# Attention maxima as one paced stream, P @ V two pieces behind its scores, and four gate tiles kept for the first merges, in a hybrid encoder layer

## The chip, the core and the metric

The kernel runs on one core of one Trainium2 chip. The metric is the device time of one execution in microseconds (us); a lower number is better. The engines are PE (TensorE, matrix products), DVE (VectorE), ACT (ScalarE), POOL (GpSimd) and SP (SyncE, which here only issues the DMAs). Each engine works through its own queue in order, and waits where an operand or a buffer isn't ready.

## What is computed

One encoder layer over 1280 tokens (1024 of a sample, 256 of a prompt), all in fp32. Cut to what matters here:

```python
h = rms_norm(x, g);  proj = h @ w_in          # split into the three mixers and three gate logits
# A: 8-head latent attention, non-causal, per request group
s = einsum('bqhd,bkhd->bhqk', q, k) * scale;  o_a = (softmax(s) @ v) @ w_o_a
# B: bidirectional RWKV-7, a scan over time for 8 heads of 64
o_b = (groupnorm(y_f + y_b) * g7) @ w_o_b
# C: 4-head attention into 256 memory tokens
o_c = (softmax(xq @ mk.T * scale) @ mv) @ w_o_c
merged = sigmoid(gate_0) * o_a + sigmoid(gate_1) * o_b + sigmoid(gate_2) * o_c
x = x + merged @ w_out
x = x + ConvFFN(rms_norm(x))
```

## The kernel before

Every fp32 product that must be exact is done as three fast products: an operand is split into a high and a low part (ACT casts the high part, POOL subtracts it for the low one, line 126 and 129), and `mm3` (lines 133 to 135) adds high*high, low*high and high*low. The 1280 tokens lie in three chunks `CH` of 512, 512 and 256 columns, numbered `ci` 0, 1, 2.

The program has two phases. Phase 1 projects h for all mixers and writes what attention and the scan need to memory. Phase 2 runs the RWKV scan (chunked into ten groups of tiles, `z` 0 to 9) with other work between its matmuls, then merges the three branches, then the output projection and the FFN.

In the first half of phase 2 the order of PE's queue is written by a planner, `Order`. Three lanes (`rwkv_chain`, `rwkv_inverse`, `rwkv_pairs`) say when their next matmuls can be ready, in planned microseconds of PE time; where none is ready, the planner takes a piece from `fill`, and when that is empty from `spare`. `fill` is first attention (a generator that yields after each piece), then the 24 gate tiles of chunk 1 (`gates`). `spare` are 16 gate tiles of chunk 0 in the list `g0`. A gate tile is 24 matmuls into one bank (PSUM tile `gt`), an evacuation by DVE (`go`, line 879) and a DMA to memory.

Of each `z` the lanes do this: for four pairs, `rwkv_decay` (PSUM tile `zz`), the Gram products (`gram`, line 1452) and the transposes (`bkt`, lines 1477 and 1480); then an inverse, most of it on DVE (from the transpose `R`, line 1507, to `P2w`, line 1562), and its products on PE (`pn`, `i`, `i32t`, then `dp` and `dd`); then two steps of the chain. A step of the chain is three groups of matmuls named `ch` (lines 1290, 1315, 1327), each of which waits for copies by ACT or DVE of the one before, with the outputs `yp` beside them.

Attention goes by items: 8 heads times 3 chunks, then 4 memory heads times 3 chunks. An item of chunk 0 or 1 has 8 pieces (blocks of 128 keys), one of chunk 2 has 2. A piece is three score matmuls (`st`, a bank of the pool `pat` with three buffers), an Exp on ACT (`pf`, line 1106), and the product with V (`ao`, line 1071; fp32, so two rows each in the profile). Scores are shifted by each query's maximum, which is found two items earlier by `neg_max`: a rough score matmul (`mx`, line 936, a bank of the same pool) and a maximum on DVE (line 937), 8 of them for an item of chunk 0 or 1, 2 for one of chunk 2; the result goes by DMA into a row of the query tile.

For each item `more()` makes two generators: `a` loads the keys and queries of the item three ahead, `b` finds the maxima of the item two ahead. After each piece `step(1)` advances both by one; after the item's last piece `rest()` runs both to their ends. The product of a piece stands in the list `late` with count 1: `unit()`, called after the next piece's Exp is issued, emits it.

The merges (`merges`) take attention's result first: `merge_in` loads four tiles (`mf`, and the reciprocals `mrd`), scales them on DVE (line 1693) and splits them into `moh`, `mol`. For each of eight output tiles `m`, `merge` multiplies with `w_o` (`woh`, `wol`, PSUM tile `mg_ps`) and applies the gate; between them stand `rwkv_out` (one of ten token tiles of the scan's output, on DVE, ACT and POOL, with four transposes `yt` on PE, line 1662), a gate tile that is kept on chip, and `gate0()`, which takes a tile that is left in `g0`. `rwkv_out` of tiles 8 and 9 stands between the merges of attention and those of the memory branch.

Of the kernel before, what the change touches and what calls it, by code (L numbers as in the profile page):

```python
# [97 lines left out]
class Kern:  # L98
# [801 lines left out]
    def spare(self, ctx, pp):  # L900

        self.gates_h(ctx[1], 0)
        self.mid = False
        yield -8.0
        while self.g0:
            self.mid = True
            for x in self.gate_(ctx[1], pp, "at", self.g0.pop(0), 0, "go", 3):
                if isinstance(x, float):
                    yield x
            self.mid = False  # L910
            yield 512 * 2.4 / 1024
# [47 lines left out]
    def attention(self, pm, tag):  # L959

        nc, io = self.nc, self.io
        with self.pool("att", side="right") as p:
# [35 lines left out]
            def ahead(h, ci):  # L998
                c0, cn = CH[ci]
                if ci == 0:  # L1000
                    e = 65 * (h % 2)
                    nc.sync.dma_start(
                        out=v1[:, :, e : e + 64], in_=io["vA"][:, :, h * 64 : (h + 1) * 64].rearrange("i p f -> p i f")
                    )
                qh, ql = queries()
                ks = []
                for c in {0: (0, 1), 1: (), 2: (2,)}[ci]:
                    cs = slice(CH[c][0], CH[c][0] + CH[c][1])
                    ks.append((io["kaT"][h][:, cs], *(k[:96, cs] for k in keys(h))))
                nxt.append((qh, ql))  # L1010
                ms = (0, NS) if c0 < NS else (NS, T)
                args = qh[:96, :cn], keys(h)[0][:96], ms, cn // 128, (qh[96:97, :cn], ql[96:97, :cn])
                mxs.append(args)
                yield from loads(*ks, (io["qT"][h][:, c0 : c0 + cn], qh[:96, :cn], ql[:96, :cn]))

            def x_ahead(h, ci):
# [10 lines left out]
                nxt.append((qh, ql, nm, self.onesr[r : r + 2]))  # L1027
                a = 0 if c0 < NS else 256
                mxs.append((qh[:, :cn], x_keys(h)[0], (a, a + 256), cn // 128, (nm[0:1, :cn], nm[1:2, :cn])))
                yield from loads(*ks)  # L1030
# [3 lines left out]
            nxt, mxs = [], []  # L1034
            for n, g in enumerate(itertools.islice(aheads, self.LOOK)):
                for _ in g:
                    pass
                if n < self.LOOK - 1:
                    for _ in self.neg_max(p, pm, tag, *mxs.pop(0)):
                        pass  # L1040
                yield
            pm, tag, po = self.pa, "at", self.po

            def more():

                a = next(aheads, iter(()))
                b = self.neg_max(p, pm, tag, *mxs.pop(0)) if mxs else iter(())

                def step(n):
                    for x in (a, *(b,) * n):  # L1050
                        next(x, None)

                def rest():
                    for x in (a, b):
                        for _ in x:
                            pass

                return step, rest
            late = []
# [33 lines left out]

            for x, h, ci in items[:24]:
                qh, ql = nxt.pop(0)
# [3 lines left out]
                ot = []  # L1099
                step, rest = more()  # L1100
                for n, kt in enumerate(kts):
# [7 lines left out]
                    args = ot, slice(0, 65), cn, v1[:, kt, e : e + 65], pf[:, :cn], kt == kts[0], kt == kts[-1]  # L1109
                    late.append([1, lambda args=args: product(*args)])  # L1110
                    if kt == kts[-1]:
                        late.append([1, lambda args=(ot, h, c0, cn): put_a(*args)])
                    step(1)
                    yield cn * 3.6 / 1024
                rest()
            while late:
                unit()
            self.recips(0, 8)
            for x, h, ci in items[24:]:
                qh, ql, nm, one = nxt.pop(0)  # L1120
# [4 lines left out]
                ot, pfs = [], []  # L1125
                step, rest = more()
                for kt in kts:
# [10 lines left out]
                    if kt == kts[-1]:  # L1138
                        late.append([1, lambda args=(ot, h, c0, cn): put_c(*args)])
                        late.append([1, lambda a=pfs[0][:, :cn], b=pfs[1][:, :cn]: nc.gpsimd.tensor_add(out=a, in0=a, in1=b)])  # L1140
                        late.append([2, lambda args=(pfs[0], h, c0, cn): den_c(*args)])
                    step(2)
                    yield cn * 4.4 / 1024
                rest()
            while late:
# [263 lines left out]
    def rwkv_prep(self, p, pr, gr, j, st):  # L1409
# [45 lines left out]
        for e in range(2):  # L1455
# [4 lines left out]
            for q in range(2):  # L1460
# [6 lines left out]
                )  # L1467
        self.od.pe(1.2, "pr", 2.7)
        yield
# [255 lines left out]
    def merges(self, gp, ro, mg, pp, merged):  # L1725
# [358 lines left out]
```

## Time and profile before

| | us |
|---|---|
| Median of three runs | 3017.24 (3015.17 to 3018.32) |
| Profiled execution, its own time | 3016.91 |
| Its span, first to last instruction | 3015.1 |
| PE busy in the span | 2796.7 (93%) |
| DVE busy | 1546.9 (51%) |
| POOL busy | 1352.4 (45%) |
| ACT busy | 1173.7 (39%) |

The profile gives, for one execution, the busy time of each engine, and in stretches of the span the clock that was granted to TensorE (1 is 2.4 GHz, 0.5 is 1.2 GHz, a figure between them is the mean of a stretch). A timeline has one row for a run of like instructions: start, length, engine, line, tile written and tiles read, and in square brackets the idle time just before it with what ended it. A view of waits adds such idle times by pair of waiter and releaser. Lengths of matmuls overlap, since they are pipelined; the distance between two starts is what a matmul costs the queue.

### The profile page before, as it was taken

To read this page: it belongs to the slowest core of one execution; us is meant where nothing else is said; L and a number is where in the kernel's file an instruction comes from. 1 tells how busy PE (TensorE), PEld (TensorE's weight loads), DVE (VectorE), ACT (ScalarE), POOL (GpSimd) and SP (SyncE) were. 2 spreads that over 40 slices of the span, in tenths; PEclk is the share of its full clock that TensorE was granted. 3 is DMA by queue.
4 is the path that set the end of the run, shared out by engine and by line. 5 is a ranking of instruction groups with operands and counts; after the bars stand their busy time and mean duration, and the time that the engine had idled before them with its cause. 6 is when DMAs were issued, how large, how long until landed. Compare 5 with 4: busy or idle time off the path is not lost.

```text
span 3015.1 us, 50261 instructions
## 1 busy us (share of the span) xinstructions
PE 2796.7 (93%) x19556; PEld 2244.5 (74%) x19556; DVE 1546.9 (51%) x2576; ACT 1173.7 (39%) x2561; POOL 1352.4 (45%) x1220
## 2 busy tenths in 40 slices
PE   6998998998888988989989598999999999999999
PEld 5787787885555665567767476888888888888888
DVE  8638858665666566755665365423423223233233
ACT  5645454635545545554443233433221111211111
POOL 5546636453433433545544366843433332433322
PEclk9999998998989989999989799999999999999999
DMA  4233224553122222243333665532111111111112
GB/s 152 95 97 104 86 79 119 137 149 83 46 54 55 60 55 68 78 136 106 106 118 103 183 190 167 167 97 72 44 37 36 43 35 43 36 42 39 34 38 84
DMA packets 250005, 261.77 MB, mean 87 GB/s; under 512 B 81028, under 2 KB 178448, under 8 KB 249768
## 3 DMA queue, kind: packets, MB, share of 16 engines
q1 hardware_dynamic: 249768, 258.57, 29.1%
q8 instruction: 154, 2.52, 0.3%
q14 instruction: 83, 0.68, 0.1%
HBM read 196.64 MB, written 61.73 MB: 86 GB/s over the span
## 4 chain that ended last, share of the span: by engine, by line
PE 43%; DVE 3%; DMA 3%; issue 2%; POOL 2%; ACT 1%; SPq 1%; DVEq 0%; POOLq 0%; ACTq 0%
PE up L133 7%; PE up L134 7%; PE up L135 7%; PE dn L133 3%; PE dn L134 3%; PE dn L135 3%; PE gt L133 2%; PE gt L134 1%; PE gt L135 1%; PE wo_ps L133 1%; PE wo_ps L135 1%; PE wo_ps L134 1%; DMA mg<-s_gT 1%; POOL w4l L129 1%; PE mg_ps L134 1%
## 5 line engine op out<-in xcount | busy, mean ns | idle before, releaser
L133 PE MATMUL up<-h2h,wuh 128*128 128x512 f32 (+1 forms) x1056 | 374.2, 354 | 0.0
L134 PE MATMUL up<-h2h,wul 128*128 128x512 f32 (+1 forms) x1056 | 374.0, 354 | 0.0
L135 PE MATMUL up<-h2l,wuh 128*128 128x512 f32 (+1 forms) x1056 | 373.5, 354 | 0.0
L129 POOL TENSOR_TENSOR w4l<-w4f,w4h 128x512 fp32r<-128x512 f32 (+1 forms) x154 | 265.2, 1730 | 210.9 <-ACT w4h L126 197.5
L129 POOL TENSOR_TENSOR wul<-wuf,wuh 128x1024 fp32r<-128x1024 f32 x52 | 125.1, 2406 | 270.4 <-ACT wuh L126 270.4
L133 PEld LDWEIGHTS up<-h2h,wuh 128*128 128x128 f32 x1056 | 199.7, 189 | 27.9
L135 PEld LDWEIGHTS up<-h2l,wuh 128*128 128x128 f32 x1056 | 199.6, 189 | 27.8
L134 PEld LDWEIGHTS up<-h2h,wul 128*128 128x128 f32 x1056 | 199.7, 189 | 27.4
L1832 DVE TENSOR_TENSOR x<-x,dn 128x512 f32<-128x512 f32 (+1 forms) x192 | 113.6, 598 | 194.3 <-PE dn L135 194.3
L133 PE MATMUL proj<-hh,w4h 128*128 128x512 f32 (+1 forms) x504 | 181.8, 362 | 9.0 <-DVE go L879 5.0
L134 PE MATMUL dn<-ah,wdl 128*128 128x256 f32 (+1 forms) x528 | 187.2, 356 | 0.0
L135 PE MATMUL dn<-al,wdh 128*128 128x256 f32 (+1 forms) x528 | 184.7, 356 | 0.0
L133 PE MATMUL dn<-ah,wdh 128*128 128x256 f32 (+1 forms) x528 | 182.1, 356 | 0.4 <-ACT wdh L126 0.4
L134 PE MATMUL proj<-hh,w4l 128*128 128x512 f32 (+1 forms) x504 | 180.5, 358 | 1.1 <-POOL w4l L129 1.1
L135 PE MATMUL proj<-hl,w4h 128*128 128x512 f32 (+1 forms) x504 | 180.9, 359 | 0.0
L133 PE MATMUL gt<-ghh,w4h 128*128 128x512 f32 x384 | 162.5, 423 | 13.0 <-ACT w4h L126 6.0
L1071 PE MATMUL ao<-pf,va 128*65 128x512 f32 (+1 forms) x288 | 152.8, 614 | 22.8 <-ACT pf L1106 15.1
L126 ACT CAST wuh<-wuf 128x1024 fp32r<-128x1024 f32 x52 | 54.7, 1051 | 291.3 <-PE up L135 276.1
L1852 DVE TENSOR_TENSOR fraw<-up,rbc 128x512 f32<-128x512 f32 (+1 forms) x66 | 39.8, 604 | 247.7 <-PE up L135 241.0
L126 ACT CAST w4h<-w4f 128x512 fp32r<-128x512 f32 (+1 forms) x154 | 113.2, 750 | 136.5 <-DMA w4f<-in_w_g 35.4
L129 POOL TENSOR_TENSOR wdl<-wdf,wdh 128x384 fp32r<-128x384 f32 (+1 forms) x64 | 60.3, 944 | 225.1 <-ACT wdh L126 225.1
L134 PE MATMUL gt<-ghh,w4l 128*128 128x512 f32 x384 | 154.8, 403 | 5.0 <-POOL w4l L129 5.0
(392 smaller groups left out, 7382.5 us busy)
## 6 DMA issues: line engine op xcount, KB each, us to landing
w4f<-in_w_g SPq DMA_DIRECT2D x48, 512.0 KB
wuf<-in_w_up SPq DMA_DIRECT2D x44, 512.0 KB
rk<-s_rk SPq DMA_DIRECT2D x80, 192.0 KB
w4f<-in_w_g SPq DMA_DIRECT2D x48, 256.0 KB
s_gT<-go SPq DMA_DIRECT2D x40, 256.0 KB
mg<-s_gT SPq DMA_DIRECT2D x40, 256.0 KB
wdf<-in_w_down SPq DMA_DIRECT2D x48, 192.0 KB
w4f<-in_w_rw SPq DMA_DIRECT2D x30, 256.0 KB
```

Source lines behind the costliest of these rows:

```text
L126: nc.scalar.copy(out=hi, in_=x)
L129: (nc.gpsimd if el == "pool" else nc.vector).tensor_sub(out=lo, in0=x, in1=hi.bitcast(F32))
L133: mm(ps, lhsT=lh, rhs=rh, start=first, stop=False)
L134: mm(ps, lhsT=ll, rhs=rh, start=False, stop=False)
L135: mm(ps, lhsT=lh, rhs=rl, start=False, stop=last)
L1071: nc.tensor.matmul(ot[0][out, :cn], lhsT=lhsT, rhs=rhs, start=start, stop=stop)
L1832: nc.vector.tensor_add(out=xc, in0=xc, in1=ps[:, :cn])
L1852: nc.vector.tensor_mul(out=raw[:, o : o + cn], in0=ps, in1=self.rbc[:, c0 : c0 + cn])
```

## The change

Six edits:

1. `more()` with its `step` and `rest` is gone. One stream runs the maxima of all items: `step(a, n)` advances the loads by one and adds n to a credit (at most 2), and each whole credit advances the running `neg_max` by one maximum, whichever item it belongs to. n is 1.15 per piece of the heads and 2.0 per piece of the memory heads. `ready(i)` runs the stream as far as item i needs before its first piece.
2. An item's maxima are entered in the list `mxs` after its loads are issued, no longer before, and the DMA for V follows the loads.
3. A product and what follows it (`put_a`) stand in `late` with count 2 instead of 1, for the eight heads; the memory heads keep 1.
4. The first pair of the scan is planned at 9.0 us instead of 0, and the bank of a Gram product is held 3.4 planned us instead of 2.7.
5. `spare` stops while four tiles are left in `g0`, and the merges take these four before the first `merge_w`.
6. `rwkv_out` of tiles 8 and 9 moves behind the start of the first two merges of the memory branch.

```diff
-        while self.g0:
+        while len(self.g0) > 4:
...
+                yield from loads(*ks, (io["qT"][h][:, c0 : c0 + cn], qh[:96, :cn], ql[:96, :cn]))
                 mxs.append(args)
-                yield from loads(*ks, (io["qT"][h][:, c0 : c0 + cn], qh[:96, :cn], ql[:96, :cn]))
+                if ci == 0:
+                    e = 65 * (h % 2)
+                    nc.sync.dma_start(
...
-            def more():
-
-                a = next(aheads, iter(()))
-                b = self.neg_max(p, pm, tag, *mxs.pop(0)) if mxs else iter(())
...
+            pace = [0.0, None]
+
+            def step(a, n):
+
+                next(a, None)
+                pace[0] = min(pace[0] + n, 2.0)
+                while pace[0] >= 1.0:
+                    if pace[1] is None:
+                        if not mxs:
+                            return
+                        pace[1] = self.neg_max(p, pm, tag, *mxs.pop(0))
+                    try:
+                        next(pace[1])
+                        pace[0] -= 1.0
+                    except StopIteration:
+                        pace[1] = None
+                        done.append(0)
+
+            def ready(i):
+
+                while len(done) <= i:
+                    pace[0] = 1.0
+                    step(iter(()), 0.0)
...
-                    late.append([1, lambda args=args: product(*args)])
+                    late.append([2, lambda args=args: product(*args)])
                     if kt == kts[-1]:
-                        late.append([1, lambda args=(ot, h, c0, cn): put_a(*args)])
-                    step(1)
+                        late.append([2, lambda args=(ot, h, c0, cn): put_a(*args)])
+                    step(a, 1.15)
                     yield cn * 3.6 / 1024
-                rest()
+                for _ in a:
+                    pass
...
-                    step(2)
+                    step(a, 2.0)
...
-                yield "pr", lambda: 0.0 if z < 2 else od.when(f"c{z - 2}")
+                yield "pr", lambda: (0.0 if n else 9.0) if z < 2 else od.when(f"c{z - 2}")
...
-        self.od.pe(1.2, "pr", 2.7)
+        self.od.pe(1.2, "pr", 3.4)
...
         for m in range(8):
+            if m == 0:
+                for _ in range(4):
+                    gate0()
             w = self.merge_w(mg, 0, m)
...
-        self.rwkv_out(ro, pp, 8)
-        self.rwkv_out(ro, pp, 9)
         for m in range(8):
+            if m < 2:
+                self.rwkv_out(ro, pp, 8 + m)
```

What this does to the queues, at three places. First, PE at the end of an item of chunk 2, here the second head's. Before (`st` are scores, `ao` products with V, `mx` maxima, `zz` and `gram` belong to the scan):

```order
L133 MATMUL st<-aqh,akb_5961 128x256
L134 MATMUL st<-aqh,akb_5961 128x256
L135 MATMUL st<-aql,akb_5961 128x256
L1071 MATMUL ao<-pf,va 65x256
L936 MATMUL mx<-akb_5960,aqh 128x512 x7
L133 MATMUL st<-aqh,akb_5960 128x512
L134 MATMUL st<-aqh,akb_5960 128x512
L135 MATMUL st<-aql,akb_5960 128x512
L1071 MATMUL ao<-pf,va 65x256
```

The same place of PE's queue now:

```order
L133 MATMUL st<-aqh,akb_5960 128x256
L134 MATMUL st<-aqh,akb_5960 128x256
L135 MATMUL st<-aql,akb_5960 128x256
L1081 MATMUL ao<-pf,va 65x512
L936 MATMUL mx<-akb_5961,aqh 128x256 x2
L133 MATMUL st<-aqh,akb_5961 128x512
L134 MATMUL st<-aqh,akb_5961 128x512
L135 MATMUL st<-aql,akb_5961 128x512
L1081 MATMUL ao<-pf,va 65x256
```

The seven maxima in a row are gone (there were seven such rows in the program, and now there is no row of more than two behind the start of phase 2), and the product behind a piece is that of two pieces before.

Second, PE at the end of the scan, from the last two groups of its last chain to the first merge (`gt` are gate tiles). Before:

```order
L133 MATMUL gt<-ghh,w4h 128x512
L1327 MATMUL ch_17982<-W,bkt 64x64 x16
L1336 MATMUL yp<-W,g_16189 64x64 x4
L1336 MATMUL yp<-W,g_16190 64x64 x4
L1336 MATMUL yp<-W,g_16191 64x64 x4
L1336 MATMUL yp<-W,g_16192 64x64 x4
L134 MATMUL gt<-ghh,w4l 128x512
L135 MATMUL gt<-ghl,w4h 128x512
L133 MATMUL gt<-ghh,w4h 128x512
L134 MATMUL gt<-ghh,w4l 128x512
L135 MATMUL gt<-ghl,w4h 128x512
L133 MATMUL mg_ps<-moh,woh 128x512
```

And now, from the last chain's last step on:

```order
L1304 MATMUL ch_17916<-W,agr 64x64 x16
L1312 MATMUL yp<-sd,agr 64x128 x8
L1329 MATMUL ch_17947<-xs,Tt_6469 64x64 x16
L1341 MATMUL ch_17966<-W,bkt 64x64 x16
L1350 MATMUL yp<-W,g_16257 64x64 x4
L1350 MATMUL yp<-W,g_16258 64x64 x4
L1350 MATMUL yp<-W,g_16259 64x64 x4
L1350 MATMUL yp<-W,g_16260 64x64 x4
L133 MATMUL gt<-ghh,w4h 128x512
L134 MATMUL gt<-ghh,w4l 128x512
L135 MATMUL gt<-ghl,w4h 128x512
```

From the last `dp` to the first merge there were 87 gate matmuls, between the chain's groups; now there is none among them, and four tiles (96 gate matmuls, ten merge matmuls among the last of them) follow the last `yp`. Three tiles (72 matmuls) that stood in the merges of `m` 0, 1 and 2 are gone from there, and 63 more gate matmuls stand ahead of that `dp`.

Third, POOL at the entry of the merges (`w4l` splits a gate tile's weights, `mol` and `wol` the merges' operands). Before:

```order
L129 TENSOR_TENSOR w4l<-w4f,w4h 128x1024 x3
L129 TENSOR_TENSOR mol<-mf,moh 128x256
L129 TENSOR_TENSOR wol<-wof,woh 128x512
L129 TENSOR_TENSOR mol<-mf,moh 128x512
L129 TENSOR_TENSOR mol<-mf,moh 128x256
L129 TENSOR_TENSOR mol<-mf,moh 128x512
```

And now:

```order
L1318 TENSOR_TENSOR sw<-sd,wc 64x512 x2
L129 TENSOR_TENSOR mol<-mf,moh 128x256
L129 TENSOR_TENSOR wol<-wof,woh 128x512
L129 TENSOR_TENSOR w4l<-w4f,w4h 128x1024
L129 TENSOR_TENSOR mol<-mf,moh 128x512
L129 TENSOR_TENSOR w4l<-w4f,w4h 128x1024
L129 TENSOR_TENSOR mol<-mf,moh 128x256
```

The weights of the third and fourth kept tile are split between the first tiles of attention's result.

## Rows read from the trace of the kernel before

**Rows 1.** Busy time by stretch of the span: heads, and entry of the merges.
```profile
core 0: us, PE busy (x) PEld busy (x) DVE busy (x) ACT busy (x) POOL busy (x), PEclk, DMA share, GB/s
684.20:1184.50 500.30, 448.63 (x4307) 289.25 (x4308) 316.85 (x707) 265.37 (x777) 192.46 (x204) 0.91 0.22 57
...
1683.40:1728.20 44.80, 12.11 (x27) 6.42 (x25) 18.29 (x30) 10.94 (x20) 17.82 (x15) 0.55 0.72 213
```

**Rows 2.** Waits of PE from 676 to 1184.5 us, largest pairs.
```profile
engine line waited for: us in total, times, longest us
PE mx L936 <- DVE m L937: 16.4, 11, 3.3
PE ao L1071 <- ACT pf L1106: 15.1, 19, 2.6
PE zz L1372 <- DMA lt<-s_lora: 7.7, 1, 7.7
...
PE ao L1071 <- DVE P2w L1562: 3.6, 1, 3.6
```

**Rows 3.** The seven rows of seven maxima, by stretch: line 936 alone.
```profile
core 0: us, PE busy (x) PEld busy (x), PEclk, DMA share, GB/s
...
780.20:789.60 9.40, 4.18 (x7) 2.08 (x7) 0.66 0.31 91
...
sum 44.70, PE 26.24 PEld 14.15; mean PE 3.75 PEld 2.02
```

**Rows 4.** Timeline of PE: a piece with a maximum, one without.
```profile
763.21 0.48 PE L133 MATMUL st<-aqh,akb 97*128 97x512 f32 x1
...
763.99 1.02 PE L1071 MATMUL ao<-pf,va 128*65 128x512 f32 x2
764.45 0.79 PE L936 MATMUL mx<-akb,aqh 96*128 96x512 f32 x1
765.08 0.40 PE L133 MATMUL st<-aqh,akb 97*128 97x512 f32 x1
...
696.59 0.80 PE L133 MATMUL st<-aqh,akb 97*128 97x512 f32 x1
...
698.15 0.80 PE L133 MATMUL st<-aqh,akb 97*128 97x512 f32 x1
```

**Rows 5.** The six stretches at half clock that begin in such a row.
```profile
855.00:868.60 13.60, 12.59 (x33) 7.86 (x34) 12.05 (x48) 4.82 (x12) 0.73 (x1) 0.50 0.35 84
...
sum 57.80, PE 50.86 PEld 33.02 DVE 47.94 ACT 13.62 POOL 17.23; mean PE 8.48 PEld 5.50 DVE 7.99 ACT 2.27 POOL 2.87
```

**Rows 6.** Three of five items of chunk 1, a maximum behind each piece.
```profile
705.40:726.00 20.60, 19.53 (x109) 12.22 (x105) 12.07 (x22) 13.68 (x43) 10.16 (x11) 1.00 0.17 46
754.60:776.40 21.80, 20.19 (x111) 12.22 (x110) 18.94 (x53) 14.17 (x49) 9.53 (x11) 1.00 0.14 43
...
1085.40:1121.30 35.90, 34.71 (x622) 25.49 (x620) 19.48 (x36) 21.69 (x66) 12.63 (x16) 1.00 0.15 39
```

**Rows 7.** Timeline: a chain step of the ninth group, then the last chain.
```profile
1596.87 1.15 PE L1290 MATMUL ch<-W,agr 128*64 128x64 f32 x32
...
1599.92 1.15 PE L1315 MATMUL ch<-xs,Tt 64*64 64x64 f32 x32
...
1603.28 1.15 PE L1327 MATMUL ch<-W,bkt 128*64 128x64 f32 x32
...
1605.98 0.42 DVE L1286 COPY W<-sd 64x512 f32<-64x512 f32 x1
...
1655.91 1.15 PE L1290 MATMUL ch<-W,agr 128*64 128x64 f32 x32 [0.30 <-DVE Tt L1627]
...
1681.30 1.10 PE L1336 MATMUL yp<-W,g 128*64 128x64 f32 x32
...
1728.18 1.12 PE L1662 MATMUL yt<-ident,oy 128*128 128x128 f32 x4 [3.56 <-DVE oy L1658]
```

**Rows 8.** Timeline of PE: one gate tile, first row and the row behind it.
```profile
1738.81 0.39 PE L133 MATMUL gt<-ghh,w4h 128*128 128x512 f32 x1
...
1744.29 0.39 PE L133 MATMUL mg_ps<-moh,woh 128*128 128x512 f32 x1
```

**Rows 9.** Timeline of PE: the transposes of the tenth token tile.
```profile
1867.82 1.12 PE L1662 MATMUL yt<-ident,oy 128*128 128x128 f32 x4 [11.29 <-DVE oy L1658]
```

**Rows 10.** Timeline of POOL: the low part of one gate tile's weights.
```profile
1684.96 2.34 POOL L129 TENSOR_TENSOR w4l<-w4f,w4h 128x1024 fp32r<-128x1024 f32 x1 [5.28 <-ACT w4h L126]
```

More of the change, by code (lines that the diff above doesn't have):

```diff
@@ L999, in ahead @@
                 c0, cn = CH[ci]
[L1000 to L1004, printed above, removed]
                 qh, ql = queries()
@@ L1012, in ahead @@
                 args = qh[:96, :cn], keys(h)[0][:96], ms, cn // 128, (qh[96:97, :cn], ql[96:97, :cn])
+                yield from loads(*ks, (io["qT"][h][:, c0 : c0 + cn], qh[:96, :cn], ql[:96, :cn]))
                 mxs.append(args)
-                yield from loads(*ks, (io["qT"][h][:, c0 : c0 + cn], qh[:96, :cn], ql[:96, :cn]))
+                if ci == 0:
+                    e = 65 * (h % 2)
+                    nc.sync.dma_start(
+                        out=v1[:, :, e : e + 64], in_=io["vA"][:, :, h * 64 : (h + 1) * 64].rearrange("i p f -> p i f")
+                    )
             def x_ahead(h, ci):
@@ L1028, in x_ahead @@
                 a = 0 if c0 < NS else 256
+                yield from loads(*ks)
                 mxs.append((qh[:, :cn], x_keys(h)[0], (a, a + 256), cn // 128, (nm[0:1, :cn], nm[1:2, :cn])))
-                yield from loads(*ks)
             items = [(x, h, ci) for x, n in ((0, 8), (1, 4)) for h in range(n) for ci in range(3)]
             aheads = iter([(x_ahead if x else ahead)(h, ci) for x, h, ci in items])
-            nxt, mxs = [], []
+            nxt, mxs, done = [], [], []
             for n, g in enumerate(itertools.islice(aheads, self.LOOK)):
@@ L1040, in attention @@
                         pass
+                    done.append(0)
                 yield
             pm, tag, po = self.pa, "at", self.po
-            def more():
-                a = next(aheads, iter(()))
-                b = self.neg_max(p, pm, tag, *mxs.pop(0)) if mxs else iter(())
[L1049 to L1058, printed above, removed]
+            pace = [0.0, None]
[12 more added lines that the diff above has]
+                        pace[1] = None
+                        done.append(0)
+            def ready(i):
+                while len(done) <= i:
+                    pace[0] = 1.0
+                    step(iter(()), 0.0)
             late = []
@@ L1092, in den_c @@
                 nc.sync.dma_start(out=io["den"][8 + h : 9 + h, c0 : c0 + cn], in_=ds[0:1, :cn])
-            for x, h, ci in items[:24]:
+            for i, (x, h, ci) in enumerate(items[:24]):
+                ready(i)
                 qh, ql = nxt.pop(0)
@@ L1099, in attention @@
                 ot = []
-                step, rest = more()
+                a = next(aheads, iter(()))
                 for n, kt in enumerate(kts):
@@ L1118, in attention @@
             self.recips(0, 8)
-            for x, h, ci in items[24:]:
+            for i, (x, h, ci) in enumerate(items[24:], 24):
+                ready(i)
                 qh, ql, nm, one = nxt.pop(0)
@@ L1125, in attention @@
                 ot, pfs = [], []
-                step, rest = more()
+                a = next(aheads, iter(()))
                 for kt in kts:
@@ L1141, in attention @@
                         late.append([2, lambda args=(pfs[0], h, c0, cn): den_c(*args)])
-                    step(2)
+                    step(a, 2.0)
                     yield cn * 4.4 / 1024
-                rest()
+                for _ in a:
+                    pass
             while late:
```

## The prediction

> **What bounds the kernel now.** I read four things in this order. The time by stretch comes first: PE is busy nearly all the time, so what can be won is where it isn't, or where its clock is low. In the heads' stretch, 500.3 us, PE is busy for 448.6 and has a mean clock of 0.91 [rows 1]. At the entry of the merges, 44.8 us, it is busy for 12.1 at 0.55 [rows 1]. The rest of the span is not touched, and I leave it as it is. Second, the waits in the heads: PE waits 16.4 us for DVE's maxima, 15.1 for the Exp of a piece before its product, 7.7 once for the first load of the scan [rows 2]. Third, the rows of seven maxima, where the first of these waits sits: seven of them take 44.7 us [rows 3]. Fourth, the clock beside them: of the stretches at half clock in the heads, six, together 57.8 us, begin in one of these rows [rows 5], while five items of chunk 1, in which a maximum follows each piece, ran at 1.00 throughout [rows 6]. So PE's own queue sets the time here, through bursts that DVE can't keep up with and through the clock behind them.
>
> The sum is made against the profiled execution's 3016.9 us (its span and 1.8 beside it), which is 0.3 below the median of the three runs; about 0.2%, 6 us, is what a measurement of this kernel can tell from no change.
>
> **The change part by part.**
>
> *The start.* PE waits 7.73 us for the scan's first load [rows 2]. Planned at 9 us, that load's matmuls stand behind four attention pieces, whose inputs were loaded in phase 1. What then hides it is the pieces; if their banks come free late it is hidden in part. Between 0 and -7.7 I take **-6.5**.
>
> *The paced maxima.* A piece with a maximum takes 765.08 - 763.21 = 1.87 us, one without 698.15 - 696.59 = 1.56 [rows 4]: a maximum between pieces costs 0.31. The 49 maxima of the seven bursts, 44.7 us [rows 3], then cost 49 x 0.31 = 15; those that stand in twos cost a little more, so -29 becomes **-26**. If DVE is as late for spread maxima as for bunched ones, nothing comes of it; the ends are 0 and -29.
>
> *The clock.* A mean of 0.91 over 500.3 us [rows 1] is 90 us at half clock, which cost at most half of that. Of the 57.8 us that begin in bursts [rows 5], some 21 lie in the bursts (counted above) and 36 behind them, so 18 us were lost there. I take 14 of these, and 4 for the low stretch that begins in the wait at the start: **-18**, with ends of -5 and -35 (then the other low stretches go too). What rows say for it: the items with a maximum behind each piece kept 1.00, with PE busy 19.5 of 20.6 us and 34.7 of 35.9 [rows 6].
>
> The Trainium skill has a rule that speaks against this (TensorE: Matmul & The Clock Gate, section "A second HAM failure mode: psum-queue depth-cycling"): a kernel that cycles through PSUM banks in each iteration idles in small gaps often enough that the clock swings between its two levels. Scores and maxima do cycle through three banks here. By that rule this term would be 0; by the row it is -18. The trace disagrees with the rule for this pattern: 1.00 in all five items.
>
> *P @ V two pieces behind.* The product no longer waits for the Exp just issued; 15.1 us of such waits in 19 places [rows 2]. But the pool has three banks, and scores and maxima take them in turn: the maximum behind piece n+1 takes the bank of piece n, and so waits for the same Exp, only a product later, 764.45 - 763.99 = 0.46 us [rows 4]. So each wait shrinks by 0.46 at most and moves from `ao` to `mx`: 19 x 0.46 = 8.7, less the waits that were smaller, **-7**; ends 0 and -15.
>
> *The fuller queues.* What is won from PE's queue makes DVE and ACT denser: DVE was busy 316.9 of 500.3 us in the heads [rows 1], and in one item during an inverse 18.9 of 21.8 [rows 6]. Each piece now hangs on a maximum, also in the pieces of chunk 0, which mostly had none while DVE did the inverse. The nearest row is PE's one wait for the inverse, 3.6 us [rows 2]; at two or three such waits for the five groups that lie in the heads, I add **+12**, ends 0 and +30.
>
> *Longer hold of a Gram bank, loads before maxima, V behind the loads.* Pieces are 1.8 planned us, so a hold of 2.7 or 3.4 is mostly two pieces either way; the V load on SP's queue waits for a product that is two pieces later, with 8 pieces to spare. I cost these at nothing; what covers them is attention itself.
>
> *The last chain and the entry.* A gate tile is 1744.29 - 1738.81 = 5.48 us [rows 8], 0.228 a matmul. The order has 63 more gate matmuls ahead of the last `dp`: +14.4. The last chain took 1681.30 - 1655.91 = 25.4 us with gates in it [rows 7]. Bare, a step is about 2.0 to its second group (the 3.05 of the rows less the Gram product that stood between), 3.36 to the third, and 3.1 to the end of the copy for the next step [rows 7], 8.5 in all; to the last `yp` it is 8.5 + 2.0 + 3.4 + 1.0 = 14.9. So the chain ends 14.4 - 10.5 = 3.9 later in PE's work. From there to the first `yt` it was 46.9 us, nearly all loading [rows 7]; the loads start at the chain's end as before, and the four tiles, 22 us, now lie under them. POOL gets two splits of 2.34 between the merges' own [rows 10]: up to +4.7, I take +2. Then three tiles, 3 x 5.48 = 16.4, no longer stand in the merges; as the merges behind them get shorter their own loads show, and I give back 2. Sum 3.9 + 2 - 16.4 + 2, about **-9**; ends -16 and +6.
>
> *Token tiles 8 and 9.* PE stood 11.29 us before the second one's transposes [rows 9]. Now 24 merge matmuls stand ahead of them, some 4.6 us of work that is done inside the wait; what is late next is the last tiles of the memory branch, so **-3.5**, ends 0 and -4.6.
>
> Sum: -6.5 - 26 - 18 - 7 + 12 - 9 - 3.5 = **-58**, so 3016.9 - 58 = **2959 us**.
>
> **The rivals.**
>
> *DVE takes the place of the burst.* DVE's queue is in order, and a maximum behind the inverse's operations is late for each piece and not only in a burst. For it: 18.9 of 21.8 us busy in an item [rows 6]. Against it: that same item lost hardly anything, with PE busy 20.2 of 21.8. Then the pacing gives half, the later product nothing, and the fuller queues cost 24: -58 + 13 + 7 + 12 = -26, **2991 us**.
>
> *The clock stays as it is.* Three banks in turn make small gaps everywhere, and the heads stay at 0.91: without the clock's 18 and with 3 more for the slower start, -37, **2980 us**. Against it stands 1.00 in five items [rows 6]. This is what the rule named above gives.
>
> *More comes than I count.* All low stretches of the heads go (-35), the Exp waits too (-15), nothing is given back by DVE: -58 - 17 - 8 - 12, and a bit less at the ends, **2922 us**.
>
> *Slower.* The inverse itself becomes the bound. Its DVE operations stand in order with the maxima, thirteen or so of them in its time; if they stretch it beyond PE's time from `R` to `pn`, PE stands before `pn`, and the chain, the pairs and the loads behind it with it. It decides from about 12 us per group over five groups on top of the 12 I count, plus the clock lost in each gap: 58 + 15, **3032 us**. Against it: one single wait of 3.6 us for the inverse in the heads [rows 2].
>
> **How the numbers follow.** My forecast has 0.62, DVE's place 0.17, the clock 0.05, more 0.10, slower 0.06. The forecast's own range is 2935 to 2985. The range 2922 to 2997 takes in the clock's case, most of DVE's and part of the better one; it leaves out slower (0.06) and about 0.12 at the two ends. Faster by over 0.2%: the first four less the far end of DVE's, 0.91; within it 0.03; slower 0.06.
>
> **What would show it.** After the change the waits `mx` for DVE should be under 6 us in the heads, the clock there 0.97 or more, the wait for the scan's first load gone, Exp waits partly under `mx`. The heads' stretch, 500.3 us [rows 1], should take some 460. At the entry PE should be busy for 30 us or more, and the last chain should show gaps of 1 to 2 us between its groups. The longest wait of `yt` should fall below 8. I am wrong if the low stretches stay without the bursts, if `st` or `mx` wait for DVE in each item, or if the wait for the inverse comes back in each group.

## The result and the profile after

The changed kernel takes 2967.78 us (median of four runs, 2966.98 to 2974.26); the kernel before, measured beside it, 3016.66. The ratio is 0.9843, with a 95% interval of 0.9825 to 0.9860: 49 us less, where 58 were forecast. The profiled run has a span of 2966.6 us.

The stretches, PE alone (length, busy time and instructions, mean granted clock, DMA): from the end of phase 1 to the start of the scan, heads, memory heads, gates up to the last `dp`, last chain, from there to the first `yt`, merges.

```profile
670.60:681.30 10.70, 7.41 (x29) 1.00 0.67 195
681.30:1126.60 445.30, 410.45 (x4176) 0.95 0.24 63
1126.60:1248.30 121.70, 111.09 (x1028) 0.86 0.26 76
1248.30:1627.00 378.70, 350.23 (x4180) 0.94 0.37 113
1627.00:1647.70 20.70, 12.90 (x354) 0.92 0.17 53
1647.70:1698.60 50.90, 29.39 (x123) 0.81 0.72 220
1698.60:1935.90 237.30, 220.23 (x1073) 0.96 0.60 178
```

The same stretches of the kernel before:

```profile
676.40:684.20 7.80, 0.07 (x3) 0.79 1.00 293
684.20:1184.50 500.30, 448.63 (x4307) 0.91 0.22 57
1184.50:1297.70 113.20, 103.35 (x1207) 1.00 0.28 81
1297.70:1651.10 353.40, 325.00 (x3834) 0.94 0.38 114
1651.10:1682.40 31.30, 31.00 (x435) 1.00 0.32 100
1682.40:1728.20 45.80, 13.11 (x31) 0.56 0.71 210
1728.20:1984.40 256.20, 233.76 (x1145) 0.97 0.57 171
```

Start and heads together went from 508.1 to 456.0 us (-52.1), the memory heads from 113.2 to 121.7 (+8.5, at a clock of 0.86 that was 1.00), the gates from 353.4 to 378.7 (+25.3), the last chain from 31.3 to 20.7 (-10.6), the way to the first `yt` from 45.8 to 50.9 (+5.1), the merges from 256.2 to 237.3 (-18.9). Phase 1 was 5.8 shorter; what follows the merges took 1030.7 in both. Not all of the heads' 52 us is won: in the gates' stretch PE has 346 instructions more. 63 of them are gate matmuls; the others are one inverse's products (256) and a pair's decay and transposes (28), which used to lie among the attention's pieces; by the distances between such groups in the timeline they are some 9 us of work. Only a part of that stood in the heads: with 16 Gram products that went into the memory heads, some 5 us. The rest left the memory heads, which have 179 instructions less and still take longer.

What PE waited for in the heads, largest pairs (to be read against [rows 2]):

```profile
engine line waited for: us in total, times, longest us
PE ao L1081 <- ACT os L1085: 13.7, 7, 5.2
PE mx L936 <- DVE m L937: 8.0, 5, 3.0
PE st L133 <- ACT pf L1117: 6.4, 5, 2.1
PE zz L1386 <- DMA lt<-s_lora: 3.3, 1, 3.3
```

The waits of a product for its Exp are gone from the list (15.1 us before). In their place stands a pair that was small in the kernel before, a product for `os`:

```profile
PE ao L1071 <- ACT os L1075: 3.8, 3, 2.3
```

There is one bank for `ao`; ACT empties it into `os` when an item is done, and the next item's first product needs it. The longest of these waits, on ACT:

```profile
1119.34 0.38 ACT L1117 ACTIVATE pf<-st 128x256 f32<-128x256 f32 x1
1123.93 0.20 ACT L1477 COPY dblk<-gram 32x64 f32<-32x64 f32 x1 [4.22 <-DVE agr L1473]
...
1124.58 0.58 ACT L1085 COPY os<-ao 65x512 f32<-65x512 f32 x1
```

And on PE at the same time:

```profile
1119.19 0.80 PE L936 MATMUL mx<-akb,aqh 128*128 128x256 f32 x2
1125.22 1.97 PE L1081 MATMUL ao<-pf,va 128*65 128x256 f32 x4 [5.23 <-ACT os L1085]
```

ACT's queue is in order. Its `dblk` waits 4.22 us for DVE's `agr`, which stands behind the inverse's operations (line 1536 is one of them):

```profile
1122.30 1.08 DVE L1536 TENSOR_TENSOR LX<-LX,tm 128x60 f32<-128x60 f32 x1
1123.42 0.43 DVE L1473 TENSOR_TENSOR agr<-gram,masks 64x256 f32<-64x256 f32 x1
```

The copy `os`, whose product PE had issued at 1118.73, is queued behind `dblk`, and PE stands 5.23 us. Right there the clock falls:

```profile
1123.20:1147.10 23.90, 21.88 (x61) 0.50 0.24 69
```

The memory heads begin at 1126.6; most of the low clock that they now show is this stretch.

### The profile page after: what moved, and what is told of

It is laid out like the page before. It is cut to its first block, busy times and chain, and to the rows that moved or that the text cites. A ratio compares the mean times of both kernels' runs of the same rounds, so it can differ in the third digit from the quotient of the medians.

```text
span 2966.6 us, 50241 instructions
## 1 busy us (share of the span) xinstructions
PE 2781.4 (94%) x19556; PEld 2246.2 (76%) x19556; DVE 1544.2 (52%) x2576; ACT 1173.3 (40%) x2561; POOL 1358.5 (46%) x1220
## 5 line engine op out<-in xcount | busy, mean ns | idle before, releaser
L126 ACT CAST w4h<-w4f 128x512 fp32r<-128x512 f32 (+1 forms) x154 | 113.2, 751 | 149.6 <-DMA w4f<-in_w_g 41.1
L937 DVE TENSOR_REDUCE m<-mx 128x1 f32<-128x512 f32 (+1 forms) x184 | 107.6, 601 | 105.7 <-PE mx L936 105.1
```

The costliest lines, as they stand in the source:

```text
L126: nc.scalar.copy(out=hi, in_=x)
L937: nc.vector.tensor_reduce(out=m2[:, n, z : z + 1], in_=ps[:, :kn], axis=AX.X, op=ALU.max)
```

## The experiments

All were timed beside the kernel before, which had a median of 3017 to 3019 us; so the ratios are the better comparison. Where the text gives a difference of medians and the ratios say something else, both stand.

| kernel | us, median (range) | ratio (interval) |
|---|---|---|
| changed | 2967.8 (2967.0 to 2974.3) | 0.9843 (0.9825 to 0.9860) |
| changed, product one behind | 2965.6 (2964.5 to 2968.1) | 0.9824 (0.9811 to 0.9837) |
| changed, maxima as before | 2981.4 (2977.8 to 2985.9) | 0.9877 (0.9861 to 0.9894) |
| before, paced maxima alone | 2996.4 (2990.9 to 3002.6) | 0.9925 (0.9911 to 0.9940) |
| changed, last product one behind | 2961.1 (2956.1 to 2966.0) | 0.9808 (0.9792 to 0.9823) |
| changed, start at 0 | 2975.1 (2971.6 to 2982.1) | 0.9862 (0.9846 to 0.9878) |
| changed, Gram bank 2.7 | 2975.3 (2970.5 to 2979.8) | 0.9855 (0.9838 to 0.9871) |
| changed, no kept gate tiles | 2969.9 (2964.0 to 2977.4) | 0.9843 (0.9824 to 0.9863) |
| changed, token tiles 8 and 9 as before | 2963.9 (2962.8 to 2968.5) | 0.9825 (0.9810 to 0.9840) |
| before, planner's two numbers alone | 3007.9 (3000.0 to 3012.3) | 0.9963 (0.9951 to 0.9976) |
| before, pacing and the two numbers | 2965.4 (2964.5 to 2967.6) | 0.9826 (0.9810 to 0.9842) |
| last product one behind, token tiles as before | 2961.1 (2958.1 to 2964.6) | 0.9811 (0.9794 to 0.9828) |
| the same, 1.0 maxima for a piece | 2957.0 (2954.4 to 2958.8) | 0.9800 (0.9784 to 0.9816) |

**The product one piece behind again.**

```diff
-                    late.append([2, lambda args=args: product(*args)])
+                    late.append([1, lambda args=args: product(*args)])
...
-                        late.append([2, lambda args=(ot, h, c0, cn): put_a(*args)])
+                        late.append([1, lambda args=(ot, h, c0, cn): put_a(*args)])
```

> The changed kernel with the product and put_a one piece behind its scores again (count 1); all else as changed. Theory A (the prediction's term): the later product was worth 7 us, so 2968 + 7 = 2975 us, with some 13 us of PE waits of ao for the Exp pf back. Theory B (read from the trace after the change): nothing was won, because the wait moved. There ao waits 13.7 us for the copy os that empties its only bank (3.8 before) and st waits 6.4 us for pf; together 20.1 us, where before ao for pf, ao for os and mx for pf were 20.9. Then this run takes 2964 to 2972 us, with ao for os back under 5. Theory C: with a maximum behind every piece count 1 hurts more than it did before, and the clock with it: 2985 us or more.

2965.6 us: theory B on the time, so beside the other edits the later product is worth nothing that can be measured. PE's waits in the heads:

```profile
PE ao L1081 <- ACT os L1085: 12.3, 8, 4.6
PE ao L1081 <- ACT pf L1117: 8.9, 14, 1.1
PE st L133 <- DVE m L937: 8.5, 6, 4.7
PE st L133 <- ACT pf L1117: 3.5, 5, 2.1
```

B's reason is wrong in one point: `os` is waited for with count 1 as well, 12.3 us. It comes with the new place that the planner's numbers give the scan's groups, not with the count and not with the pacing: it is 3.5 us with pacing alone, and 10.8 with the two numbers alone (both below). The waits of a product for its Exp are back, 8.9 us in 14 places, but the longest is 1.1 us, and the run isn't longer.

**The maxima as before, all else as changed.**

```diff
-                    step(a, 1.15)
+                    step(1)
...
-                for _ in a:
-                    pass
+                rest()
```

(with `more()` back and `ready(i)` gone)

> The changed kernel with the maxima taken as before (two generators for each item, run to their ends behind its last piece); all else as changed, the product two pieces behind too. Theory A (the prediction's terms): pacing gives 26 us of queue and 14 us of clock behind the bursts, and costs some 12 in fuller queues: 2968 + 28 = 2996 us, with the mean clock of the heads back at 0.91 to 0.92. Theory B: the low clock comes from the waits at the ends of the items of chunk 2 whatever the maxima do, so only the queue's part returns: 2982 us and a clock of 0.94 or more in the heads.

2981.4 us, which is B: 14 us for pacing in this surrounding by the medians, 10 by the ratios, whose intervals just don't overlap. The bursts bring back 13.6 us of `mx` for DVE in the heads (8.0 in the changed kernel), and the heads' stretch, start included, is 464.6 us where it was 456.0:

```profile
669.50:1134.10 464.60, 426.41 (x4201) 0.94 0.25 65
```

```profile
PE mx L936 <- DVE m L937: 13.6, 12, 3.2
```

**Pacing alone.** Edits 1 and 2 on the kernel before.

> The kernel before with the paced maxima and the order of loads alone (edits 1 and 2); product one behind, start at 0, Gram bank, gate tiles and token tiles as before. Theory A (the prediction's terms): 3017 - 26 - 14 + 12 = 2989 us. Theory B (pacing needs the later product, since now each piece has its maximum and the Exp comes later): less than half of it, 3003 us or more, with more than 20 us of waits of ao for pf in the heads.

2996.4 us, 23 below before (by the ratio 0.9925): midway between the two. B's sign, more than 20 us of `ao` for `pf`, isn't there (13.4). The heads with the start, and the waits there:

```profile
674.80:1159.10 484.30, 431.49 (x4312) 0.94 0.24 63
```

```profile
PE ao L1081 <- ACT pf L1117: 13.4, 16, 2.4
PE mx L936 <- DVE m L937: 8.7, 5, 4.0
PE zz L1386 <- DMA lt<-s_lora: 8.1, 1, 8.1
PE st L133 <- ACT pf L1117: 7.1, 7, 2.6
PE ao L1081 <- ACT os L1085: 3.5, 3, 1.5
PE st L133 <- DVE m L937: 3.5, 7, 1.1
```

Before, PE was idle for 59.4 us of 508.1 here, now for 52.8 of 484.3. So the bursts' waits were mostly traded: `mx` and `st` for DVE fell from 17.9 to 12.2 us, but `st` for the Exp came up with 7.1. What pacing did give is the clock: a mean of 0.91 over 500 us is at most 45 us lost, 0.94 over 484 at most 29, so 16 less. PE's busy time says the same: for nearly the same instructions (4308 and 4312) it fell by 17.2 us, from 448.7 to 431.5.

**The last product of an item one behind.**

```diff
-                    late.append([2, lambda args=args: product(*args)])
+                    late.append([1 if kt == kts[-1] else 2, lambda args=args: product(*args)])
...
-                        late.append([2, lambda args=(ot, h, c0, cn): put_a(*args)])
+                        late.append([1, lambda args=(ot, h, c0, cn): put_a(*args)])
```

> The changed kernel with one edit: the last product of an item and its put_a stand one piece behind, the others two. Theory B of the first run says why: the copy os stands in ACT's in-order queue behind dblk, which waits for the scan's agr on DVE (4.2 us at 1119.7, then ao 5.2), and the one bank of ao is held so long. Issued a piece earlier it is ahead of the next item's first product by two pieces: waits of ao for os from 13.7 us to under 5, and less low clock behind them: 2968 - 9 - 5 = 2954 us. Rival: the last product then waits for its Exp instead, or the bank was not what held PE, and it is the start of the next item (st for pf) that waits longer: 2964 to 2972 us.

2961.1 us, ratio 0.9808, with an interval that ends just below where that of the changed kernel begins: a gain of some 7 us by the medians, half of the 14 expected, and 11 by the ratios. The waits:

```profile
PE st L133 <- DVE m L937: 10.0, 7, 4.1
PE mx L936 <- DVE m L937: 8.1, 6, 3.8
PE st L133 <- ACT pf L1117: 3.8, 3, 2.5
```

The pair `ao` for `os` is gone, as expected. But DVE's maxima are late instead, 18.1 us against 9.8. The longest of these waits, 4.1 us, ends at 943.7, where in the changed kernel `ao` waited 4.0 us for `os` (until 944.8): DVE has the inverse's operations ahead of the maximum there, and once the bank is free the next thing that PE needs from DVE ends last.

**The first pair at 0 again.**

```diff
-                yield "pr", lambda: (0.0 if n else 9.0) if z < 2 else od.when(f"c{z - 2}")
+                yield "pr", lambda: 0.0 if z < 2 else od.when(f"c{z - 2}")
```

> The changed kernel with the first pair of the scan planned at 0 again instead of 9.0 us; all else as changed. Theory A (the prediction's term): PE waits 7 to 8 us for the scan's first load again, and a low clock behind it costs some 4: 2968 + 8 = 2976 us. Theory C (from the run with the old maxima, where the heads' stretch stayed 43.5 us below before without any pacing): the two numbers of the planner, this one and the hold of the Gram bank, carry a good part of the heads' gain, because they put the scan's groups elsewhere among the pieces: 2982 us or more. Theory D: the wait is only traded for another at the start: 2965 to 2971 us.

2975.1 us, theory A on the time: 7 us by the medians, 6 by the ratios, whose intervals overlap. PE waits 7.9 us for the load again (3.3 in the changed kernel). In the order, the three gate tiles that had come in ahead of the last `dp` move back into the last chain (63 matmuls), and with them the inverse's products and the pair move back among the attention's pieces: the heads, start included, have 4311 instructions again where the changed kernel has 4203. So the run undoes more than the wait.

**The Gram bank held 2.7 again.**

```diff
-        self.od.pe(1.2, "pr", 3.4)
+        self.od.pe(1.2, "pr", 2.7)
```

> The changed kernel with the Gram bank held for 2.7 planned us again instead of 3.4; all else as changed. Theory A (the prediction cost it at nothing, since pieces of 1.8 planned us make both holds two pieces): 2965 to 2971 us. Theory C (the same as for the start: the planner's numbers carry what pacing and the later product don't): 2976 us or more, with the waits of bkt for loff and agr, 2.6 us in the heads before and none among the larger ones after, back at 5 us or more.

2975.3 us: about 7 by the medians, 4 by the ratios, whose intervals overlap. That it costs nothing isn't borne out, though it isn't excluded either; theory C's waits of `bkt` did not come back among the larger ones.

**No kept gate tiles.**

```diff
-        while len(self.g0) > 4:
+        while self.g0:
...
-            if m == 0:
-                for _ in range(4):
-                    gate0()
```

> The changed kernel without the four kept gate tiles (the planner may use all of the 16, the merges start as before); all else as changed, token tiles 8 and 9 too. Theory A (the prediction's term of -9): 2977 us, with the last chain at some 31 us instead of 20.7, the stretch of the gates 14 us shorter, and the merges 16 longer. The stretches of the trace after, less the token tiles, give 2974. Rival: POOL's splits at the entry (5.1 us more of it after) eat the gain, so that it is worth nothing: 2965 to 2971 us.

2969.9 us, ratio 0.9843: the rival on the time, but not for its reason alone. The last chain is 31.3 us long again and the way to the first `yt` 46.6, but the merges take 233.8 and not 16 more. The count of gate matmuls in PE's written queue tells why:

| gate matmuls | ahead of the last `dp` | to the last `yp` | to the first `yt` | behind it |
|---|---|---|---|---|
| before | 1377 | 82 | 5 | 264 |
| changed | 1440 | 0 | 96 | 192 |
| changed, no kept tiles | 1449 | 82 | 5 | 192 |
| before, the two numbers alone | 1449 | 82 | 5 | 192 |
| changed, start at 0 | 1377 | 63 | 96 | 192 |
| changed, Gram bank 2.7 | 1425 | 15 | 96 | 192 |

In this run the three tiles left the merges (264 to 192) because of the planner's two numbers: with them it takes three more of the spare tiles, as it does in the kernel before with the numbers alone. But edit 5 takes them out as well: the planner had left three tiles before, edit 5 makes it leave four, and all four go to the entry. So either edit is enough, and a run that undoes one of the two can't show what moving these tiles is worth; edit 5 alone on the kernel before was not run. What this run does show is the rest of edit 5: it carries 91 matmuls to the entry, 82 of them from the last chain.

**Token tiles 8 and 9 as before.**

```diff
-            if m < 2:
-                self.rwkv_out(ro, pp, 8 + m)
...
+        self.rwkv_out(ro, pp, 8)
+        self.rwkv_out(ro, pp, 9)
         for m in range(8):
```

> The changed kernel with token tiles 8 and 9 ahead of the memory branch's merges again; all else as changed. Theory A (the prediction's term of -3.5, from a wait of 11.3 us before the tenth tile's transposes, of which 4.6 are covered): 2971.5 us, with a wait of yt of 10 us or more instead of 1.75. Rival (the wait that was seen, 11.3 to 1.75, is what it gives): 2977 us. Second rival: the time is set by the loads of the branch and comes back there: 2966 to 2969 us.

2963.9 us, which is below the changed kernel, with overlapping intervals: no gain of this edit can be measured. The tenth tile's transposes, with the tiles as before, and in the changed kernel:

```profile
1809.54 1.11 PE L1676 MATMUL yt<-ident,oy 128*128 128x128 f32 x4 [8.54 <-DVE oy L1672]
```

```profile
1818.94 0.66 PE L1676 MATMUL yt<-ident,oy 128*128 128x128 f32 x4 [1.75 <-DVE oy L1672]
```

The wait did shrink by 6.8 us, more than the 4.6 that were counted as cover. But the merges behind it wait 4.8 us for ACT's `moh` in the changed kernel, and not at all without the edit:

```profile
PE yt L1676 <- DVE oy L1672: 15.1, 3, 6.9
PE mg_ps L133 <- ACT moh L126: 4.8, 3, 3.1
```

The merges as a whole are 2.4 us shorter with the edit (237.3 against 239.7).

**The planner's two numbers alone.** Both numbers of the change in the kernel before, nothing else.

> The kernel before with the planner's two numbers alone (first pair at 9.0 us, Gram bank held 3.4). In its order the planner takes three gate tiles more ahead of the last dp, and the three that stood in the merges are gone, without any tile being kept. Theory A (the prediction's terms: start -6.5, its clock -4, hold 0, three tiles moved at no gain): 3017 - 10 = 3007 us. Theory C (from the runs without the pacing, 35 us below before, and with start or hold undone, 7 us each): these numbers carry some 25 us by themselves, in part because three tiles leave the merges, where loads keep PE waiting, for the gates' stretch: 2992 us.

3007.9 us, 9 below before by the medians and 11 by the ratio: theory A to the microsecond, though not by its terms, so the hit is luck. The heads with the start, the gates and the merges:

```profile
675.20:1158.20 483.00, 431.63 (x4200) 0.93 0.24 63
...
1278.80:1662.70 383.90, 353.18 (x4190) 0.95 0.37 112
...
1740.60:1977.10 236.50, 218.81 (x1073) 0.96 0.59 176
```

The merges are 20 us shorter and the heads 25, but the gates 30 longer and the memory heads 7: tiles and scan work have changed places, and 7 us are left of it in this profile. Two of the waits in the heads:

```profile
PE ao L1071 <- ACT os L1075: 10.8, 5, 5.0
PE ao L1071 <- ACT pf L1106: 8.6, 13, 1.5
```

This run also shows what edits 3, 5 and 6 and the order of the loads do where there is no pacing. The changed kernel with the maxima as before has all of these beside the two numbers, and is at 0.9877 where the numbers alone are at 0.9963: 26 us. 18 of them lie in the heads (483.0 to 464.6), where of these edits only the later product and the order of the loads act, and the waits of a product for its Exp, 8.6 us here, are not among that run's waits.

**Pacing and the two numbers.** Edits 1, 2 and 4 on the kernel before.

> The kernel before with the paced maxima, the order of loads and the planner's two numbers; product one behind, no kept gate tiles, token tiles 8 and 9 as before. Theory A (the prediction's terms for what is left out: product 7, last chain and entry 9, token tiles 3.5): 2968 + 19 = 2987 us. Theory C (each of the three edits left out gave 2 us or less when it was undone alone): 2963 to 2973 us.

2965.4 us, theory C: as fast as the whole change. Edits 3, 5 and 6 together give nothing that can be measured once there is pacing. Its stretches, last chain, way to the first `yt`, merges:

```profile
1624.80:1656.10 31.30, 31.00 (x436) 1.00 0.33 101
1656.10:1701.50 45.40, 13.13 (x32) 0.57 0.71 211
1701.50:1932.90 231.40, 217.56 (x1073) 0.97 0.60 180
```

308.1 us from the last `dp` to the end of the merges, against 308.9 in the changed kernel: the chain is 10.6 longer, what follows 5.5 and 5.9 shorter.

**Two versions beyond the change.** The last product one behind and the token tiles as before; and the same with

```diff
-                    step(a, 1.15)
+                    step(a, 1.0)
```

> The changed kernel with the last product of an item and its put_a one piece behind, and token tiles 8 and 9 ahead of the memory branch's merges as before. If the two gains seen apart (7 us and 4 us) are both real and independent: 2957 us. If the second was scatter: 2961 us.

> As the run before it, with 1.0 maxima for each piece of the heads instead of 1.15 (18 pieces of three items need 18 maxima, so 1.0 keeps up). Theory: the waits that are left in the heads are for DVE's maxima (18 us with the last product one behind), and two maxima in a row are where they fall; without the doubles 6 us of it go: 2951 us. Rival: the waits are set by what DVE does for the scan at the ends of the items, and the same maxima wait there, only singly: 2955 to 2960 us.

2961.1 and 2957.0 us. The first is what was expected if the token tiles' 4 us were scatter: they add nothing to the last product's gain. The second lies in the rival's range and not at 2951, though the waits for DVE's maxima did shrink. With 1.0 the heads, start included, take 440.4 us, and PE's waits for DVE's maxima there are 10.2 us (18.1 with 1.15):

```profile
PE st L133 <- DVE m L937: 7.8, 10, 2.2
...
PE mx L936 <- DVE m L937: 2.4, 4, 0.8
```

The step from 1.15 to 1.0 is 4 us by medians, with overlapping intervals. The kernel as a whole, at 0.9800 (0.9784 to 0.9816), is faster than the changed one.

## Why the prediction was right, and where its steps were not

The time lies within the range and 9 us from the forecast. The sum held better than its terms, and that is luck in good part, as the end of this section shows. Of the signs that were named, the gaps in the last chain and `yt` below 8 us came (0.8 to 1.5 us between the groups of its two steps, and 6.9), and PE is busy for 29.4 us at the entry where 30 was named; but `mx` waits 8.0 us for DVE in the heads and not under 6, the clock in the heads is 0.95 and not 0.97, the wait for the first load isn't gone, and the Exp is waited for by `st`.

*The start*, forecast -6.5, and -4 of the clock's -18: the size fits, but isn't clear of the noise. Undone, it costs 7 us (6 by the ratios, with overlapping intervals), and that run moves tiles and scan work too; the wait for the load went from 7.7 to 3.3 us and not to nothing.

*The paced maxima and the clock*, forecast -26, -14 of the clock, and +12 for fuller queues, so -28: alone they gave 23. Of that the clock gave 16 to 17 us in the heads. In the forecast it had the 14 behind the bursts, and up to 10 more inside -26, for the 21 us at low clock that lie in the bursts; so its size is borne out, though the heads of the changed kernel show 0.95. The rule of the Trainium skill that was weighed there (TensorE: Matmul & The Clock Gate, section "A second HAM failure mode: psum-queue depth-cycling"), which the page tells of one other kernel, would have left the clock at 0.91. With a maximum behind nearly every piece, in turn through the same three banks, the clock rose, to 0.94 with pacing alone, so the traces go against the rule here too. The queue's part came out within its forecast, but by other waits than the step named: what is left of -26 and the +12 make -4 to -14 of idle time, and PE's idle time in the heads fell by 6.6 us. The three banks were tied to the Exp as before, and a maximum behind each piece made PE wait for ACT (`st` for the Exp, 7.1 us) where it had waited for DVE (17.9 to 12.2 us).

*P @ V two pieces behind*, forecast -7: 0 beside the pacing. Without the pacing it is hardly 0: there it and the order of the loads together take 18 us out of the heads, by one profile each, and the waits of a product for its Exp, 8.6 us, are gone. By itself on the kernel before it was not run. The step said that the wait would move to `mx` less 0.46 us each; it moved to `st` (6.4 us). The one bank of `ao` and ACT's in-order queue were not in the step at all, and they are what holds PE longest in the heads now (13.7 us). The rival of DVE's place had the mechanism nearer, only that DVE holds PE through ACT: `dblk` waits for `agr`, and `os` behind it.

*The longer hold of the Gram bank*, forecast 0: for the hold by itself this stays open (7 us by the medians, 4 by the ratios, within the noise). What failed is the step under both numbers: each was costed by the one wait or bank that it concerns, and the order that the planner makes of them was not. Together they moved the scan's groups against the pieces and had the planner take three spare tiles more. On the kernel before the two numbers are worth 9 us, on the paced one 31 (2996.4 to 2965.4).

*The last chain and the entry*, forecast -9: 2 by the medians and 0 by the ratios (the run without kept tiles). The bare chain was worked out well: 14.9 us from its first group to the last `yp`, and it was 14.7 (31.3 to 20.7 for the stretch). But the three tiles (+14.4 ahead of the last `dp`, -16.4 in the merges) were put down to the kept tiles, and the planner's numbers move them too. Without them the step would have read -10.5 for the chain and 4 given back. Against the run without kept tiles the chain is 10.6 shorter, the entry 4.3 and the merges 3.5 longer: what is given back, 7.8, was the term that was too small.

*Token tiles*, forecast -3.5: not measurable; what is late next is `moh`, which was not named.

So three of the six edits, the pacing with its order of loads (1 and 2) and the planner's numbers (4), give the whole gain, and more together than apart: 23 and 9 alone, 52 together. They are enough, but not the only way: with the numbers and without pacing, the other edits take 26 us of the 43 that pacing takes there (3007.9 to 2965.4), so they remove much of the same time.

Why the two are worth 20 us more together isn't settled. From pacing alone to both, the profiles have 32 us less in the heads, 6 more in the memory heads, 19 more in the gates and 27 less in the merges; from before to the numbers alone 25, 7, 30 and 20. Work changes places between heads, memory heads and gates, so their sum says more: it grows by 12.8 us with the numbers on the kernel before (974.7 to 987.5) and shrinks by 6.7 on the paced one (957.6 to 950.9), with the same 72 gate matmuls more. That difference, 19.5 us, is most of what the profiles show (30; the profiled execution of pacing alone was the slowest of its five), so the joint gain arises in the main ahead of the last `dp`. PE's idle time there falls by 2.9 us in the one case and by 14.2 in the other, and its busy time grows by 15.7 and by 6.3. So part of it is idle time and part is clock; which wait lets go is open, and these are single profiles.

The errors of the sum nearly cancelled: 5 us too much for pacing, clock and queues (28 against 23), 1.5 for the numbers alone (10.5 against 9), 7 for the product, 9 for the entry, 3.5 for the token tiles; and 20 too little for what comes only jointly. -58 + 26 - 20 is -52, what edits 1, 2 and 4 give.

## What to carry to other kernels

A wait that a later consumer removes is only worth what the next operand of that engine leaves: list every bank and every in-order queue that the delayed instruction still passes (here one `ao` bank and ACT's queue, stuck behind a copy for another stage) before a number is put to it. Where a planner writes the order, a change of its numbers moves work between stages, so attribute moved instructions by writing out the order with each edit alone. And a term is proved by adding the edit alone as well as by undoing it alone: here the undone edits sum to some 25 us of 49 by the medians and to 8 by the ratios, while three of them make up the whole. An edit that is worth nothing when it is undone can be worth much where another that takes the same time is absent: edits 3, 5 and 6, with the order of the loads, took 26 us without pacing, and beside it edits 3, 5 and 6 took nothing.

## What the runs showed of the chip that was not expected

The low clock follows single waits here, not only long ones. In the heads of the changed kernel PE waits 11 times for more than 1.2 us, and in ten of these places the granted clock is at its lower level by some 2 us behind the wait's end, as at 717.0, behind a wait of 1.26 us that ends at 714.97 and one of 0.62 that ends at 716.56:

```profile
717.00:720.50 3.50, 3.50 (x22) 0.51 0.24 46
```

The length of a wait alone doesn't decide it here: in the kernel before, the clock fell at 11 of 15 such waits, and the four where it stayed were 1.30 to 1.76 us long.

Stretches whose queues on PE, DVE and ACT are written alike differ from run to run by several us: the heads with the start took 456.0 us in the changed kernel, 451.1 with the token tiles as before and 450.1 without kept tiles. PE's idle time in them is 38.1, 36.9 and 38.6 us, so the difference is in the busy time, at mean clocks of 0.95, 0.96 and 0.97. Phase 1, which the later edits don't reach, took 669.5 to 677.5 us in the changed kernel and its variants, while the 1030.7 us behind the merges, at a clock of 1.00, were the same in all of them. A single profile of this kernel can therefore not settle a term of 5 us, and the medians of four runs can hardly.
